# A decoder layer on one Trainium2 core: seven- and eight-product units of gate and up alternate, and a group's sums and transpositions move

## The chip, the cores and the metric

One core of one Trainium2 chip runs the whole kernel. The metric is the device time of one execution in microseconds. Three timed executions of the kernel before took 1185.75, 1186.57 and 1187.09 us; the median is 1186.57.

## The reference

One layer of a hybrid decoder on 256 tokens of width 2048, all in float32. What the change touches is the SwiGLU part, whose hidden width is 5632:

```python
def swiglu(h, w_gate, w_up, w_down):
    g = jnp.einsum('bsd,df->bsf', h, w_gate)
    u = jnp.einsum('bsd,df->bsf', h, w_up)
    return jnp.einsum('bsf,fd->bsd', jax.nn.silu(g) * u, w_down)

h = layer_norm(ALPHA * h + m, ln1_g, ln1_b)     # m: RG-LRU heads and differential attention
h = layer_norm(ALPHA * h + swiglu(h, ...), ln2_g, ln2_b)
h = layer_norm(ALPHA * h + sigmoid(h @ w_ple_gate + b) * (p @ w_ple_proj), ln3_g, ln3_b)
```

## The kernel before

**Precision.** Every float32 operand is split into two parts, hi (rounded to fp32r) and lo (what is left). A product of two matrices is three matmuls: hi by hi, hi by lo, lo by hi (`product`, L851 to L856). For the weights ScalarE casts the hi half `wh` (L159) and VectorE subtracts to get the lo half `wl` (L150). For some halves, listed in `by_dma`, VectorE is spared: ScalarE writes `wl = -wh` (L161), and a DMA issued by GpSimd adds `w` to it in place (L162).

**Stream.** All weights pass through one object, `Stream`, in units of 1 MB (128 x 2048 values). `load` (L98) issues a unit's load on SyncE's queue into one of 3 buffers `w`. A load waits until everything that read the buffer's last unit is done, and these are the casts, the subtractions and, for a `by_dma` half, GpSimd's accumulating DMA. A unit has two halves of 1024 columns, each with its `wh` and `wl` in one of 6 buffers. The program calls `tick` after each stretch of matmuls; a tick lets each running job (a generator) emit its next step and then prepares at most one lo and one hi of the stream, as long as the hi is no more than 6 halves past what the matmuls had freed a tick earlier (`room`, L166). Engines take their instructions in the order in which they were emitted.

**Gate and up.** The hidden width is cut into 11 groups of 512 columns, in three parts of 4, 4 and 3 groups (`FPARTS`), each part followed by its share of the down projection. A group has 8 units (`PAIRS`), one for each 256 rows of the contraction, with gate and up together. Five are normal units ("N" below): 8 products, 24 matmuls, a tick after each quarter (6 matmuls). Three (`SEVEN`, "S" below) are done with 7 products in place of 8, in the manner of Strassen: 21 matmuls and four ticks. They need four weight operands: the unit's first half, a block of 512 columns, and two halves of sums that VectorE makes from the loaded unit (`add_up`, L128). The order in a group is N N N N N S S S; the second halves of units 2, 3 and 4 are `by_dma`. Four PSUM banks `q[h][g]` hold plain results (token half h; g is gate or up); p1, p6, p5 and p7 hold products that enter more than one result.

**Finish.** At the first tick of the last S unit, `finish` (L912) starts: it copies the banks out, adds the products, applies SiLU, multiplies, and 3 ticks later transposes the two token halves on TensorE (L950). ScalarE and VectorE then write the transposed hi and lo into `hT`, the input of the down projection. Its steps run beside the first N units of the next group.

Of the kernel before, what the change touches and what calls it, by code (L numbers as in the profile page):

```python
# [12 lines left out]
F32R = mybir.dt.float32r  # L13
BF16 = mybir.dt.bfloat16
AF = mybir.ActivationFunctionType
ALU = mybir.AluOpType
# [4 lines left out]
P = 128  # L21
D = 2048
S = 256
KT = D // P
# [24 lines left out]
NSM = 32 + 8 * 4 + 1 + 64  # L49
PAIRS = KT // 2  # L50
SEVEN = 3


class Stream:
# [152 lines left out]
def tile_hybrid_layer(ctx: ExitStack, tc: tile.TileContext, t: dict):  # L207
    nc = tc.nc
# [3 lines left out]
    act = ctx.enter_context(tc.tile_pool(name="act", bufs=1))  # L212
# [5 lines left out]
    srcs = [t["w_a"][b] for b in range(NB)]  # L218
# [6 lines left out]
    sevens, by_dma = set(), set()  # L225
    for f0, nf in FPARTS:
        for f in range(f0, f0 + nf, 4):
            sevens.update(range(len(srcs) + PAIRS - SEVEN, len(srcs) + PAIRS))
            by_dma.update((len(srcs) + m, 1) for m in range(PAIRS - SEVEN - 3, PAIRS - SEVEN))
            srcs += [tuple(t[w][f:f + 4, :, 2 * P * j:2 * P * (j + 1)].rearrange("f p c -> p f c")  # L230
                           for w in ("w_gate", "w_up")) for j in range(PAIRS)]
        srcs += [t["w_down"][f0 // 4 + kq, blk] for kq in range(nf // 4) for blk in range(2)]
        srcs += [t["w_down"][f0 // 4 + kq, blk] for blk in range(2, 4) for kq in range(nf // 4)]
    srcs += [t["w_pg"][blk, kq] for blk in range(4) for kq in range(4)]
    after_load = {}
    st = Stream(nc, wp, srcs, after_load, sevens, by_dma)

    def bank(name):
        return pm.tile([P, 512], F32, tag="mm", name=name)

    def aux(name):
        return pa.tile([P, 512], F32, tag="aux", name=name, bufs=2)
# [81 lines left out]
    ident = const.tile([P, P], F32, name="ident")  # L324
# [28 lines left out]
    for (k0, n), x in zip(XCHUNKS, x8):  # L353
        c = slice(k0 * P, (k0 + n) * P)
# [3 lines left out]
    first = [bank("xr") for _ in range(FIRST)]  # L358
    n0 = st.take(FIRST)
    for (k0, n), x in zip(XCHUNKS, x8):  # L360
        ks = slice(k0, k0 + n)
        st.split(xhl[:, ks, :S], xhl[:, ks, S:], x)
        for u in range(FIRST):
            c = slice(k0 * P, (k0 + n) * P)
# [293 lines left out]
    for i in range(4):  # L658
        c = slice(i * 512, (i + 1) * 512)
# [8 lines left out]
    def tmp(name):  # L668
        return late.tile([P, 512], F32, tag="tmp", name=name, bufs=7)
# [142 lines left out]
    x1 = act.tile([P, KT, 2 * S], F32R, tag="B", name="x1")  # L812
    xsum = []

    def sums_of_x1():

        xsum.append(late.tile([P, SEVEN, 4, 2, P], F32R, tag="gb", name="xsum"))
        work = act.tile([P, 2 * SEVEN * 512], F32, tag="A", name="work")  # L820
        x, sums = work[:, :SEVEN * 512], work[:, SEVEN * 512:]
        ks = slice(KT - 2 * SEVEN, KT)
        nc.vector.tensor_tensor(x.rearrange("p (k s) -> p k s", s=S), x1[:, ks, :S].bitcast(F32),
# [27 lines left out]
    def product(ps, a, w, first, last):  # L851

        out = ps.rearrange("p (f c) -> p f c", c=P)
        nc.tensor.matmul(out, a[0], w[0], start=first, stop=False)  # L854
        nc.tensor.matmul(out, a[0], w[1], start=False, stop=False)  # L855
        nc.tensor.matmul(out, a[1], w[0], start=False, stop=last)  # L856

    def operand(n, j, i):

        parts = st.half(n, j)  # L860
        if n in st.sevens and j:
            return [w[:, i * 512:(i + 1) * 512].rearrange("p (f c) -> p f c", c=P) for w in parts]
        return [w.rearrange("p (f k c) -> p f k c", f=4, k=2)[:, :, i, :] for w in parts]

    def gate_up(hT, i0):

        n0 = st.take(PAIRS)  # L870
        q = [[bank("gu") for _ in range(2)] for _ in range(2)]
        for m in range(PAIRS - SEVEN):
            for g in range(2):
                for h in range(2):
                    for i in range(2):
                        k = 2 * m + i
                        a = [x1[:, k, o + h * P:o + (h + 1) * P] for o in (0, S)]
                        product(q[h][g], a, operand(n0 + m, g, i), m + i == 0,
                                g * h * i == 1 and m == PAIRS - SEVEN - 1)
                    st.free(h)  # L880
                    st.tick()
        pp = [aux("p1"), aux("p6")]
        both = pa.tile([P, 2, 512], F32, tag="sc", name="p57")
        p1, p6, p5, p7 = pp[0], pp[1], both[:, 0, :], both[:, 1, :]
        for m in range(PAIRS - SEVEN, PAIRS):
            n, first, last = n0 + m, m == PAIRS - SEVEN, m == PAIRS - 1
            def x(h, i):
                return [x1[:, 2 * m + i, o + h * P:o + (h + 1) * P] for o in (0, S)]
            def sx(i):
                return [xsum[0][:, m - PAIRS + SEVEN, i, a, :] for a in range(2)]  # L890
            product(q[0][0], x(0, 1), operand(n, 0, 1), False, last)
            product(p1, x(0, 0), operand(n, 0, 0), first, last)
            if last:
                if hT is None:
                    hT = act.tile([P, KT, 2 * S], F32R, tag="A", name="hT")
                st.start(finish(hT, i0, q, p1, p6, p5, p7))
            st.free()
            st.tick()
            product(q[0][1], sx(3), operand(n, 1, 0), False, last)
            st.free()  # L900
            product(p5, sx(0), operand(n, 2, 0), first, last)
            st.tick()
            product(p7, sx(1), operand(n, 2, 1), first, last)
            st.free()
            product(q[1][0], x(1, 1), operand(n, 3, 1), False, last)
            st.tick()
            product(p6, sx(2), operand(n, 3, 0), first, last)
            st.free()
            st.tick()
        return hT  # L910

    def finish(hT, i0, q, p1, p6, p5, p7):  # L912


        add = lambda out, a, b, op=ALU.add: nc.vector.tensor_tensor(out, a, b, op)
        yield
        g0 = tmp("g0")
        nc.scalar.copy(g0, q[0][0])
        yield
        u0, u1 = tmp("u0"), tmp("u1")  # L920
        nc.scalar.copy(u0, q[0][1])
        add(g0, p1, g0)
        nc.scalar.copy(u1, q[1][1])
        yield
        g1, u2, u3 = tmp("g1"), tmp("u2"), tmp("u3")
        nc.scalar.copy(g1, q[1][0])
        nc.scalar.copy(u2, p6)
        yield
        add(u2, p1, u2)
        nc.scalar.activation(g0, g0, AF.Silu)  # L930
        yield
        add(u3, p7, u2)
        yield
        add(u2, p5, u2)
        add(g1, g1, u3)
        yield
        add(u3, p5, u3)
        nc.scalar.activation(g1, g1, AF.Silu)
        yield
        add(u0, u0, u2, ALU.subtract)  # L940
        yield
        add(u1, u1, u3, ALU.subtract)
        add(g0, g0, u0, ALU.mult)
        yield
        add(g1, g1, u1, ALU.mult)
        yield 3
        for h, g in enumerate((g0, g1)):
            tp = aux("tp")
            for i in range(4):
                nc.tensor.transpose(tp[:, i * P:(i + 1) * P], g[:, i * P:(i + 1) * P], ident)  # L950
            yield
            tp = tp.rearrange("p (a b) -> p a b", b=P)
            hi, lo = (hT[:, i0:i0 + 4, o + h * P:o + (h + 1) * P] for o in (0, S))
            nc.scalar.copy(hi, tp)
            yield
            nc.vector.tensor_tensor(lo, tp, hi.bitcast(F32), ALU.subtract)

    for part, (f0, nf) in enumerate(FPARTS):
        hT = None
        for i0 in range(0, nf, 4):  # L960
            hT = gate_up(hT, i0)
        nq = nf // 4
        end = part == len(FPARTS) - 1
        if end:
            gb = load_gb(2)
        two = [[bank("dps") for _ in range(2)] for _ in range(2)]
        for kq in range(nq):
            for blk in range(2):
                token_major(two[blk], hT, kq, kq == 0, kq == nq - 1)
        for blk in range(4):  # L970
            if blk < 2:
                st.start(residuals(blk, two[blk], part == 0, stats if end else None), 1 + 2 * blk)
                continue
            ps = [bank("dps") for _ in range(2)]
            if end and blk == 3:
                x2 = act.tile([P, KT, 2 * S], F32R, tag="B", name="x2")
                token_major(ps, hT, 0, True, False)
                token_halves(ps, hT, (1, 2), False, True, norm_to(NORM2, x2, ps, False, stats, gb, ln_cols[2]))
                continue
            for kq in range(nq):  # L980
                token_major(ps, hT, kq, kq == 0, kq == nq - 1)
            st.start(residuals(blk, ps, part == 0, stats if end else None))
# [46 lines left out]
    n = st.take(4)  # L1029
# [126 lines left out]
```

## Time and profile before

| what | value |
|---|---|
| median of three timed executions | 1186.57 us |
| profiled execution | 1187.35 us |
| its span (first to last instruction) | 1185.6 us |
| TensorE matmul busy | 1161.7 us, 98% |
| VectorE busy | 877.7 us, 74% |
| ScalarE busy | 681.2 us, 57% |
| granted TensorE clock, mean | 0.995 |
| accumulating DMAs wl<-w | 33 of 512 KB |

The profile lists busy time by engine and by line, the chain that ended last, and waits with what released them. Matmuls overlap: each is recorded with some 0.39 us while the next starts 0.23 us after it, so a matmul's cost is the distance between two starts. A stall shorter than the overlap doesn't appear as idle time; it is seen in the starts.

### The profile page before, as it was taken

The numbers are of one execution on the slowest core, as the hardware profiler recorded it, in microseconds if no ns is written. First come the engines' busy times: TensorE is split into PE (matmuls) and PEld (weight loads), VectorE is DVE, ScalarE is ACT, GpSimd is POOL, SyncE is SP. The second block draws the span as 40 slices with busy tenths as digits, with TensorE's granted clock in tenths as the row PEclk, the third lists the DMA queues.
The fourth block names the chain that finished last, engine by engine and source line by source line (L and its number), as shares of the span: only waits on it lengthen the run. The fifth ranks groups of instructions, "written<-read, shape, count | busy, mean of one in ns | idle before, by whom it ended". The sixth has DMA issues, their size and how long they took to land.

```text
span 1185.6 us, 14774 instructions
## 1 busy us (share of the span) xinstructions
PE 1161.7 (98%) x5495; PEld 963.7 (81%) x5495; DVE 877.7 (74%) x1160; ACT 681.2 (57%) x968; POOL 65.0 (5%) x97
## 2 busy tenths in 40 slices
PE   9999999999999999999999999999999999999995
PEld 7888888888887777877888888888888888877885
DVE  6975987885667967968544887787545797866877
ACT  6767666664456747746334756764345775635540
POOL 0000000001011000000000000000000000002001
PEclk9999999999999999999999999999999999999998
DMA  9756454447738788776557779766558877846741
GB/s 327 257 223 214 146 181 172 176 144 267 274 117 259 250 225 221 242 213 249 180 207 212 199 232 266 216 219 244 191 180 228 228 232 218 315 179 220 303 150 72
DMA packets 124456, 256.29 MB, mean 216 GB/s; under 512 B 6433, under 2 KB 100553, under 8 KB 108385
## 3 DMA queue, kind: packets, MB, share of 16 engines
q1 hardware_dynamic: 116208, 221.52, 54.0%
q0 software_dynamic: 8176, 33.84, 11.8%
q8 instruction: 43, 0.70, 0.2%
q14 instruction: 29, 0.23, 0.1%
HBM read 233.82 MB, written 5.78 MB: 202 GB/s over the span
## 4 chain that ended last, share of the span: by engine, by line
PE 77%; DVE 10%; DMA 7%; issue 3%; ACT 1%; POOL 1%; SPq 0%; DVEq 0%; POOLq 0%; ACTq 0%
PE gu L856 7%; PE gu L854 7%; PE gu L855 7%; PE dps L277 6%; PE dps L279 6%; PE dps L278 6%; DMA w<-in_w_up 4%; DVE wl L150 4%; PE ops L278 2%; PE xr L251 2%; PE ops L279 2%; PE ops L277 2%; PE k L251 2%; PE yg L251 2%; DVE sums L130 2%
## 5 line engine op out<-in xcount | busy, mean ns | idle before, releaser
L159 ACT CAST wh<-w 128x1024 fp32r<-128x1024 f32 (+1 forms) x404 | 407.7, 1017 | 276.2 <-PE dps L279 117.7
L150 DVE TENSOR_TENSOR wl<-w,wh 128x1024 fp32r<-128x1024 f32 (+1 forms) x371 | 432.0, 1173 | 154.0 <-ACT wh L159 153.7
L855 PE MATMUL gu<-wl,x 128*128 128x512 f32 x506 | 197.8, 391 | 2.5 <-DVE wl L150 1.4
L854 PE MATMUL gu<-wh,x 128*128 128x512 f32 x506 | 198.9, 393 | 0.0
L856 PE MATMUL gu<-wh,x 128*128 128x512 f32 x506 | 197.3, 390 | 0.0
L277 PE MATMUL dps<-wh,hT 128*128 128x512 f32 x352 | 138.2, 393 | 1.4 <-DVE z L699 1.0
L279 PE MATMUL dps<-wh,hT 128*128 128x512 f32 x352 | 137.2, 390 | 0.0
L278 PE MATMUL dps<-wl,hT 128*128 128x512 f32 x352 | 137.2, 390 | 0.0
L855 PEld LDWEIGHTS gu<-wl,x 128*128 128x128 f32 x506 | 95.1, 188 | 23.7 <-DVE wl L150 3.1
L159 ACT CAST wh<-sums 128x1024 fp32r<-128x1024 f32 x66 | 68.9, 1052 | 76.6 <-DVE sums L130 51.5
L856 PEld LDWEIGHTS gu<-wh,x 128*128 128x128 f32 x506 | 95.1, 188 | 19.9
L854 PEld LDWEIGHTS gu<-wh,x 128*128 128x128 f32 x506 | 95.1, 188 | 19.3
L130 DVE TENSOR_TENSOR sums<-w 128x1024 f32<-128x1024 f32 x33 | 40.3, 1221 | 79.1 <-DMA w<-in_w_up 79.1
L150 DVE TENSOR_TENSOR wl<-sums,wh 128x1024 fp32r<-128x1024 f32 x66 | 77.9, 1220 | 9.8 <-ACT wh L159 9.7
L277 PEld LDWEIGHTS dps<-wh,hT 128*128 128x128 f32 x352 | 66.1, 188 | 16.6 <-issue 2.3
L279 PEld LDWEIGHTS dps<-wh,hT 128*128 128x128 f32 x352 | 66.1, 188 | 13.9
L278 PEld LDWEIGHTS dps<-wl,hT 128*128 128x128 f32 x352 | 66.2, 188 | 13.3
L162 POOL DMA_DIRECT2D wl<-w x33 | 28.5, 863 | 605.3 <-ACT wl L161 385.6
L277 PE MATMUL ops<-wh,mhl 128*128 128x512 f32 x128 | 50.4, 394 | 0.0
L278 PE MATMUL ops<-wl,mhl 128*128 128x512 f32 x128 | 49.9, 390 | 0.0
L279 PE MATMUL ops<-wh,mhl 128*128 128x512 f32 x128 | 49.9, 390 | 0.0
L251 PE MATMUL xr<-xhl,wh 128*128 128x512 f32 x128 | 47.3, 411 | 1.7 <-ACT wh L78 1.7
(257 smaller groups left out, 2008.6 us busy)
## 6 DMA issues: line engine op xcount, KB each, us to landing
w<-in_w_gate SPq DMA_DIRECT2D x88, 512.0 KB, 3.7
w<-in_w_up SPq DMA_DIRECT2D x88, 512.0 KB, 5.3
w<-in_w_down SPq DMA_DIRECT2D x44, 1024.0 KB, 4.8
w<-in_w_a SPq DMA_DIRECT2D x28, 1024.0 KB, 4.9
wl<-w POOLq DMA_DIRECT2D x33, 512.0 KB, 5.9
w<-in_w_out SPq DMA_DIRECT2D x16, 1024.0 KB, 4.8
w<-in_w_pg SPq DMA_DIRECT2D x16, 1024.0 KB, 4.9
w<-in_w_v SPq DMA_DIRECT2D x8, 1024.0 KB, 4.9
```

Of the source, the lines that this page charges most:

```text
L130: add = lambda out, a, b: self.nc.vector.tensor_tensor(out, a, b, ALU.add)
L150: self.nc.vector.tensor_tensor(wl, src, wh.bitcast(F32), ALU.subtract)
L159: self.nc.scalar.copy(self.shaped(wh, src, cols), src)
L162: self.nc.gpsimd.dma_start(wl, src, accum_op=ALU.add)
L251: nc.tensor.matmul(ps, wh[:, c], xhl[:, k, :], start=(k == 0), stop=False)
L277: nc.tensor.matmul(ps, ah, wh[:, c], start=first, stop=False)
L278: nc.tensor.matmul(ps, ah, wl[:, c], start=False, stop=False)
L279: nc.tensor.matmul(ps, al, wh[:, c], start=False, stop=last)
L854: nc.tensor.matmul(out, a[0], w[0], start=first, stop=False)
L855: nc.tensor.matmul(out, a[0], w[1], start=False, stop=False)
L856: nc.tensor.matmul(out, a[1], w[0], start=False, stop=last)
```

## The change

The units of a group come in another order. A group is now S N S N S N N N (`ORDER`); only the very first group is N N N N S N S N (`ORDER0`). In every group but the first, both halves of the N units at positions 1 and 3 are `by_dma`, and no others. The three shared products are complete after the last S unit, so `add_products` starts there: one copy and four adds. Two ticks after its adds it runs the transpositions of the group before, which were separate steps at the end of `finish`. `combine` takes the four banks out beside the last N unit, starting with its first quarter. After a part's last group the transpositions start with the sixth tick of the down projection. `hT` is taken at the second group of a part.

```diff
+ORDER = (("S", 5), ("N", 0), ("S", 6), ("N", 1), ("S", 7), ("N", 2), ("N", 3), ("N", 4))
+ORDER0 = (("N", 0), ("N", 1), ("N", 2), ("N", 3), ("S", 5), ("N", 4), ("S", 6), ("N", 7))
...
-            sevens.update(range(len(srcs) + PAIRS - SEVEN, len(srcs) + PAIRS))
-            by_dma.update((len(srcs) + m, 1) for m in range(PAIRS - SEVEN - 3, PAIRS - SEVEN))
...
+            for i, (kind, j) in enumerate(ORDER if f else ORDER0):
+                if kind == "S":
+                    sevens.add(len(srcs))
+                elif f and i in (1, 3):
+                    by_dma.update(((len(srcs), 0), (len(srcs), 1)))
...
+        for pos, (kind, m) in enumerate(order):
+            n, first, last = n0 + pos, pos == first_s, pos == last_s
+            if kind == "N":
+                for g in range(2):
+                    for h in range(2):
...
+                        if pos == PAIRS - 1 and g + h == 0:
+                            st.start(combine(q, sums))
+                        st.free(h)
+                        st.tick()
+                continue
...
             product(p6, sx(2), operand(n, 3, 0), first, last)
+            if last:
+                st.start(add_products(sums, p1, p6, p5, p7, before))
...
+    def add_products(sums, p1, p6, p5, p7, before):
+        c1, u2, u3, u4 = (sums.setdefault(i, tmp(i)) for i in ("c1", "u2", "u3", "u4"))
+        nc.scalar.copy(c1, p1)
+        yield
+        add(u2, p6, c1)
+        yield
+        add(u3, p7, u2)
+        yield
+        add(u2, p5, u2)
+        yield
+        add(u4, p5, u3)
+        if before is not None:
+            yield 2
+            yield from before
+
+    def combine(q, sums):
+        g0, g1, u0 = (sums.setdefault(i, tmp(i)) for i in ("g0", "g1", "u0"))
+        u1 = sums["u4"]
         nc.scalar.copy(g0, q[0][0])
         yield
+        nc.scalar.copy(g1, q[1][0])
+        add(g0, g0, sums["c1"])
+        yield
         nc.scalar.copy(u0, q[0][1])
+        add(g1, g1, sums["u3"])
+        yield
+        add(u1, q[1][1], u1, ALU.subtract)
         nc.scalar.activation(g0, g0, AF.Silu)
         yield
+        add(u0, u0, sums["u2"], ALU.subtract)
         nc.scalar.activation(g1, g1, AF.Silu)
         yield
         add(g0, g0, u0, ALU.mult)
         yield
         add(g1, g1, u1, ALU.mult)
...
         for i0 in range(0, nf, 4):
+            if i0 == 4:
+                hT = act.tile([P, KT, 2 * S], F32R, tag="A", name="hT")
+            before = gate_up(i0, ORDER if f0 + i0 else ORDER0, before and before(hT))
+        st.start(before(hT), 6)
```

## Rows read from the trace of the kernel before

**Rows 1.** The page: busy time by engine, and the granted clock in 40 slices.

```profile
PE 1161.7 (98%) x5495; PEld 963.7 (81%) x5495; DVE 877.7 (74%) x1160; ACT 681.2 (57%) x968; POOL 65.0 (5%) x97
PEclk9999999999999999999999999999999999999998
```

**Rows 2.** Timeline of TensorE, an N unit: start us, duration us, line, out<-in.

```profile
680.35 0.39 PE L856 MATMUL gu<-wh,x 128*128 128x512 f32 x1
680.58 0.39 PE L854 MATMUL gu<-wh,x 128*128 128x512 f32 x1
```

**Rows 3.** Chain, TensorE's transpositions (first of each pair), by start: start us, us.

```profile
682.11 0.44 PE tp L950 x4
...
724.57 0.44 PE tp L950 x4
...
809.90 0.44 PE tp L950 x4
```

**Rows 4.** Timeline of TensorE, the same transpositions for groups 0 to 3.

```profile
418.55 0.49 PE L950 MATMUL tp<-ident,g 128*128 128x128 f32 x3
...
464.36 0.49 PE L950 MATMUL tp<-ident,g 128*128 128x128 f32 x3
...
506.83 0.38 PE L950 MATMUL tp<-ident,g 128*128 128x128 f32 x2
...
551.81 0.38 PE L950 MATMUL tp<-ident,g 128*128 128x128 f32 x2
```

**Rows 5.** Timeline of TensorE, two stalls; in brackets idle time and its releaser.

```profile
446.99 0.50 PE L855 MATMUL gu<-wl,xsum 128*128 128x512 f32 x1 [0.28 <-DVE wl L150]
...
379.33 0.39 PE L854 MATMUL gu<-wh,x 128*128 128x512 f32 x1
380.74 0.50 PE L855 MATMUL gu<-wl,x 128*128 128x512 f32 x1 [1.02 <-DMA wl<-w]
```

**Rows 6.** Lines of VectorE in group 5 (668.0 to 710.5): count, busy us, mean ns.

```profile
L150 DVE TENSOR_TENSOR wl<-sums,wh 128x1024 fp32r<-128x1024 f32 x6 | 7.1, 1219 | 0.1
L130 DVE TENSOR_TENSOR sums<-sums,w 128x512 f32<-128x512 f32 x6 | 4.1, 688 | 0.1
L130 DVE TENSOR_TENSOR sums<-w 128x1024 f32<-128x1024 f32 x3 | 3.7, 1221 | 7.4 <-DMA w<-in_w_up 7.4
```

**Rows 7.** Timeline of ScalarE from the boundary of groups 4 and 5.

```profile
670.90 0.66 ACT L930 ACTIVATE g<-g 128x512 f32<-128x512 f32 x1
671.43 1.07 ACT L159 CAST wh<-w 128x1024 fp32r<-128x1024 f32 x1
672.53 1.06 ACT L161 ACTIVATE wl<-wh 128x1024 fp32r<-128x1024 f32 x1
673.50 1.04 ACT L159 CAST wh<-w 128x1024 fp32r<-128x1024 f32 x1
```

**Rows 8.** Timeline of GpSimd, the same group: the three accumulating DMAs.

```profile
673.88 0.86 POOL L162 DMA_DIRECT2D wl<-w  x1 [32.66 <-PE gu L855]
677.39 0.86 POOL L162 DMA_DIRECT2D wl<-w  x1 [2.64 <-ACT wl L161]
681.86 0.86 POOL L162 DMA_DIRECT2D wl<-w  x1 [3.61 <-ACT wl L161]
```

**Rows 9.** Timeline of SyncE's queue, the same stretch: the loads.

```profile
678.95 0.37 SPq L105 DMA_DIRECT2D w<-in_w_gate  x1
...
683.45 0.37 SPq L105 DMA_DIRECT2D w<-in_w_gate  x1
...
689.92 0.37 SPq L105 DMA_DIRECT2D w<-in_w_gate  x1
```

**Rows 10.** Waits of SyncE's queue: us in total, times, longest us.

```profile
SPq L105 <- DMA wl<-w: 162.9, 33, 9.1
```

**Rows 11.** Tile wl on GpSimd: issue to landing of all 33.

```profile
DMA to landing us min/median/max: 4.5/5.9/10.8
```

**Rows 12.** Chain before the stalls of group 3: start us, us, what.

```profile
505.14 10.67 DMA w<-in_w_up
```

More of the change, by code (lines that the diff above doesn't have):

```diff
@@ L227, in tile_hybrid_layer @@
         for f in range(f0, f0 + nf, 4):
-            sevens.update(range(len(srcs) + PAIRS - SEVEN, len(srcs) + PAIRS))
-            by_dma.update((len(srcs) + m, 1) for m in range(PAIRS - SEVEN - 3, PAIRS - SEVEN))
-            srcs += [tuple(t[w][f:f + 4, :, 2 * P * j:2 * P * (j + 1)].rearrange("f p c -> p f c")
-                           for w in ("w_gate", "w_up")) for j in range(PAIRS)]
+            for i, (kind, j) in enumerate(ORDER if f else ORDER0):
[3 more added lines that the diff above has]
+                    by_dma.update(((len(srcs), 0), (len(srcs), 1)))
+                srcs.append(tuple(t[w][f:f + 4, :, 2 * P * j:2 * P * (j + 1)].rearrange("f p c -> p f c")
+                                  for w in ("w_gate", "w_up")))
         srcs += [t["w_down"][f0 // 4 + kq, blk] for kq in range(nf // 4) for blk in range(2)]
@@ L863, in operand, with gate_up @@
         return [w.rearrange("p (f k c) -> p f k c", f=4, k=2)[:, :, i, :] for w in parts]
-    def gate_up(hT, i0):
+    def gate_up(i0, order, before):
         n0 = st.take(PAIRS)
         q = [[bank("gu") for _ in range(2)] for _ in range(2)]
[L872 to L881, printed above, removed]
         pp = [aux("p1"), aux("p6")]
@@ L884, in gate_up @@
         p1, p6, p5, p7 = pp[0], pp[1], both[:, 0, :], both[:, 1, :]
-        for m in range(PAIRS - SEVEN, PAIRS):
-            n, first, last = n0 + m, m == PAIRS - SEVEN, m == PAIRS - 1
+        kinds = [kind for kind, _ in order]
+        first_s, last_s = kinds.index("S"), PAIRS - 1 - kinds[::-1].index("S")
+        sums = {}
+        for pos, (kind, m) in enumerate(order):
[3 more added lines that the diff above has]
+                    for h in range(2):
+                        for i in range(2):
+                            a = [x1[:, 2 * m + i, o + h * P:o + (h + 1) * P] for o in (0, S)]
+                            product(q[h][g], a, operand(n, g, i), pos + i == 0 or (pos == 1 and first_s == 0 and
+                                    (h, g) == (1, 1) and i == 0), pos == PAIRS - 1 and i == 1)
+                        if pos == PAIRS - 1 and g + h == 0:
[3 more added lines that the diff above has]
+                continue
             def x(h, i):
@@ L890, in sx @@
                 return [xsum[0][:, m - PAIRS + SEVEN, i, a, :] for a in range(2)]
-            product(q[0][0], x(0, 1), operand(n, 0, 1), False, last)
+            product(q[0][0], x(0, 1), operand(n, 0, 1), pos == 0, False)
             product(p1, x(0, 0), operand(n, 0, 0), first, last)
[L893 to L896, printed above, removed]
             st.free()
             st.tick()
-            product(q[0][1], sx(3), operand(n, 1, 0), False, last)
+            product(q[0][1], sx(3), operand(n, 1, 0), pos == 0, False)
             st.free()
@@ L904, in gate_up, with add @@
             st.free()
-            product(q[1][0], x(1, 1), operand(n, 3, 1), False, last)
+            product(q[1][0], x(1, 1), operand(n, 3, 1), pos == 0, False)
             st.tick()
             product(p6, sx(2), operand(n, 3, 0), first, last)
+            if last:
+                st.start(add_products(sums, p1, p6, p5, p7, before))
             st.free()
             st.tick()
-        return hT
-    def finish(hT, i0, q, p1, p6, p5, p7):
-        add = lambda out, a, b, op=ALU.add: nc.vector.tensor_tensor(out, a, b, op)
-        yield
[L917 to L930, printed above, removed]
+        return lambda hT: transposed(hT, i0, sums)
+    def add(out, a, b, op=ALU.add):
+        nc.vector.tensor_tensor(out, a, b, op)
+    def add_products(sums, p1, p6, p5, p7, before):
+        c1, u2, u3, u4 = (sums.setdefault(i, tmp(i)) for i in ("c1", "u2", "u3", "u4"))
+        nc.scalar.copy(c1, p1)
+        yield
+        add(u2, p6, c1)
         yield
@@ L934, in finish @@
         add(u2, p5, u2)
-        add(g1, g1, u3)
         yield
-        add(u3, p5, u3)
+        add(u4, p5, u3)
[5 more added lines that the diff above has]
+        u1 = sums["u4"]
+        nc.scalar.copy(g0, q[0][0])
+        yield
+        nc.scalar.copy(g1, q[1][0])
+        add(g0, g0, sums["c1"])
+        yield
+        nc.scalar.copy(u0, q[0][1])
+        add(g1, g1, sums["u3"])
+        yield
+        add(u1, q[1][1], u1, ALU.subtract)
+        nc.scalar.activation(g0, g0, AF.Silu)
+        yield
+        add(u0, u0, sums["u2"], ALU.subtract)
         nc.scalar.activation(g1, g1, AF.Silu)
         yield
-        add(u0, u0, u2, ALU.subtract)
-        yield
-        add(u1, u1, u3, ALU.subtract)
         add(g0, g0, u0, ALU.mult)
@@ L945, in finish, with transposed @@
         add(g1, g1, u1, ALU.mult)
-        yield 3
-        for h, g in enumerate((g0, g1)):
+    def transposed(hT, i0, sums):
+        for h, g in enumerate(("g0", "g1")):
             tp = aux("tp")
             for i in range(4):
-                nc.tensor.transpose(tp[:, i * P:(i + 1) * P], g[:, i * P:(i + 1) * P], ident)
+                nc.tensor.transpose(tp[:, i * P:(i + 1) * P], sums[g][:, i * P:(i + 1) * P], ident)
             yield
@@ L958, in tile_hybrid_layer @@
     for part, (f0, nf) in enumerate(FPARTS):
-        hT = None
+        before = None
         for i0 in range(0, nf, 4):
-            hT = gate_up(hT, i0)
+            if i0 == 4:
+                hT = act.tile([P, KT, 2 * S], F32R, tag="A", name="hT")
+            before = gate_up(i0, ORDER if f0 + i0 else ORDER0, before and before(hT))
+        st.start(before(hT), 6)
         nq = nf // 4
```

## The prediction

> **What bounds the kernel now.** I read the page first: TensorE is busy for 98% of the span and the granted clock is at its full level, 2.4 GHz, in all slices but the last, which reads 8 tenths [rows 1]. So a change that leaves the matmuls as they are can win only stalls between them. Next I read TensorE's timeline in an undisturbed unit, for the price of a matmul: the starts lie 0.225 to 0.23 us apart [rows 2]; I use 0.227. An N unit is then 24 x 0.227 = 5.44 us (a quarter 1.36), an S unit 21 x 0.227 = 4.76, and a group 5 x 5.44 + 3 x 4.76 = 41.5 plus two sets of transpositions of 0.44. The third view is the transpositions, which stand at the same place of every group and so measure its length. In the second part one group lasts 42.46 us and three together 127.79 [rows 3], 0.4 more than three times that: hardly a stall is left there. In the first part the lengths are 45.81, 42.47 and 44.98 [rows 4], so groups 1 and 3 lose 3.35 and 2.5. Last, the stalls themselves [rows 5]: in S units a matmul with `wl` waits for VectorE, and a matmul behind a wait is recorded with 0.50 us in place of 0.39, a restart of 0.11. In group 0 one wait for an accumulating DMA costs 380.74 - 379.33 - 0.227 = 1.18, with its restart 1.3; for its S units I estimate a half of what group 1 loses, 1.6. Together 2.9. Sum of what could be won: 2.9 + 3.35 + 2.5 = 8.8 us, less than 1%.
>
> **The change part by part.**
>
> Matmuls and transpositions: a group keeps 3 S and 5 N units, 183 matmuls and 8 transpositions. Nothing.
>
> The alternation. VectorE's sums and their `wl` are 7.1 + 4.1 + 3.7 = 14.9 us for three S units [rows 6], 5.0 for one, and the `wl` of its own two blocks (1024 and 512 columns, like 1.22 and 0.69 there) makes 6.9. Three in a row are 20.7 us against 14.3 of TensorE, which is how a late load turns into stalls. Alternating with an N unit whose halves go by DMA, it is 6.9 against 10.2. These stalls go. In group 0 VectorE makes two more `wl` than before (no `by_dma` there: five N units without DMA, but one fewer half before the first S), right behind the norm, so I count half of its 2.9: gain 1.5 + 3.35 + 2.5 = 7.4 (between 5 and 8.8).
>
> Finish: VectorE keeps 10 adds and products; ScalarE has one copy fewer and one more L161 (1.06 [rows 7]) for each group, 4 `by_dma` halves instead of 3. VectorE saves one `wl` (1.22). Neither engine is full; nothing by itself. The banks: the next group's first S unit rewrites q00 at once, q01 after 6 matmuls (1.36 us). The copy of q01 is done at -0.7 (below), so this is covered by 2 us; without that cover it would cost up to a copy, which I take as long as a SiLU, 0.53 between two starts [rows 7].
>
> The lead of the accumulating DMAs. This is what is late next. Before, the halves concerned are the second ones of N units and come behind other N halves: the cast is emitted some 12 us ahead of its use (first quarter of unit 0 to third quarter of unit 2). Now, by the limit of 6 halves, the cast of position 1's first half is emitted behind the third quarter of the last N unit, one quarter and one S unit before its use: 1.36 + 4.76 = 6.1 us. The other three halves have the same 6.1. The chain that must fit, from rows: start of the cast to start of L161 1.10, L161 1.06, its end to the issue 0.29 [rows 7, 8], issue to landing at least 4.5 [rows 11]: 6.95. It doesn't fit. Step by step, with t = 0 the start of a group's first S unit:
>
> - *Position 1, first half.* q01 ends at -1.36, and its copy stands ahead of the cast in ScalarE's queue: start -1.2 (a matmul ends 0.16 after the next start), step 0.53, cast at -0.67, L161 from 0.43 to 1.49, issue 1.78. Nothing else is moving then (the next load waits for this unit's DMA, below), so the landing is as for a group's first DMA, which let a load go 678.95 - 673.88 = 5.07 after its issue [rows 8, 9], some 0.1 behind the landing; between this and the shortest, 4.5, I take 4.8: 6.58. The second matmul needs it at 4.76 + 0.23 = 4.99: **1.6 late**.
> - *Second half.* Behind L161 (step 0.97 [rows 7]) stand two SiLUs of 0.53: cast at 2.46, L161 ends 4.62, issue 4.91, landing 9.71. Need 4.99 + 2.72 = 7.71: **2.0 late** in all, with two restarts of 0.11: 2.2 us a group. By the shortest landing it is 1.7 without restarts, by the median of 5.9 3.1.
> - *Position 3.* Its buffer comes free when position 1's first half is used up: 4.76 + 2.72 + 1.6 + 0.16 = 9.24; ScalarE comes to it at about 9.0 (from 4.6 on three casts of about 0.95, the last behind VectorE's second sums, which I put at 8). Cast 9.24, L161 ends 11.4, issue 11.7. By now loads move: SyncE's queue waits for the accumulating DMA of the unit whose buffer it refills (33 waits, 162.9 us before [rows 10]; in [rows 9] each of the three loads is one that waited so), so position 4's unit is issued at 9.8 and the next about 1 us later. An accumulating DMA beside such loads took 689.92 - 681.86 - 0.1 = 8.0 [rows 8, 9]; I take 7.7, between it and the median, by the nearer row: landing 19.4. Need: 4.76 + 5.44 + 4.76 + 0.23 = 15.19, and 2.2 of position 1: 17.4. **2.0 late**, with the restart 2.1. If the loads don't disturb it (4.8) it is in time: 0. If it takes 9, 3.4. Its second half lands about 22 against 22.2: nothing.
>
> The copy and the SiLUs stand ahead only where a group follows a group: 8 of 10. Where one follows the down projection (groups 4 and 8), the cast is at -2.6 and the landing at 4.7, in time; position 3 stays late by as much. Sum: 8 x 2.2 + 10 x 2.1 - 7.4 = **+31.2 us**. The profiled execution had 1187.35 (1185.6 of span and 1.75 around it), so 1218.6 on its scale; the median lies 0.8 lower: 1217.8, **1218**.
>
> A rule that bears on the landing, apart from the sum: in the Trainium skill, "DMA: Bandwidth & Descriptors", section on the anatomy of one DMA on the GpSimd path, a DMA takes about 2.0 us plus its bytes at 436 GB/s, which for 512 KB is an estimate of 3.2 us. By that, the sum would be that of the rival A below. The trace disagrees for this form: none of 33 landed under 4.5 [rows 11]. The same page (section "SWDGE vs HWDGE vs iDMA") says that each DMA engine takes turns between the queues fed by GpSimd and by the hardware generators; the 8.0 us beside loads agrees.
>
> **The rivals.**
>
> A. *The DMAs are in time, and only the stalls of S units go.* Place: position 1 and 3 of ten groups; deciding point: a loss under 7.4 / 10 = 0.74 us a group. If a landing took 3.2, position 1 would be 0.1 late in its first half and 0.4 in its second, with restarts 0.6, position 3 in time: 8 x 0.6 - 7.4 = -2.6, time 1184; with no wait at all 1179. For it: DMAs are quiet while these run. Against: the shortest landing in the trace is 4.5, and with it position 1 is still 1.7 late.
>
> B. *Position 3 isn't late.* The loads of 9.8 and 10.8 don't slow its DMA. 8 x 2.2 - 7.4 = +10: 1197. For it: second DMAs of a group, issued shortly before a load, took 683.45 - 677.39 - 0.1 = 6.0 [rows 8, 9]. Against: here two loads are issued ahead of the DMA, not behind.
>
> C. *The loads come late too.* Position 4's unit is loaded only after position 1's DMA. Beside accumulating DMAs such a load took 10.67 us, and the group that it fed is one of the stalled ones [rows 12, 4]. From 9.8 it lands at 20.5; VectorE's work up to the `wl` of the first sums is 1.22 + 1.22 + 1.38 + 0.69 + 1.22 = 5.7 [rows 6], so 26.2 against a need at 26.7 (15.19 + 4.1 of waits and restarts so far + 5.44, and 2.04 into the S unit). A spare of 0.5 us: if it goes, each group loses another 3, as groups 1 and 3 did. +31 + 30: about 1248.
>
> **How the numbers follow.** My forecast 0.58, B 0.21, C 0.13, A 0.08. The forecast's own range is 1205 to 1232 (position 1 at 1.7 to 3.3, position 3 at 1 to 3). With B below and part of C above, the range is 1194 to 1238. About 0.2% (2.4 us) is what a measurement of this kernel can tell from no change. Faster comes only from A with short landings: 0.07; same, its border, 0.02; slower 0.91: even the shortest landings with position 3 in time give 8 x 1.9 - 8.8 = +6.
>
> **What would show it.** In the profile after: waits of gu L855 for DMA wl<-w, 18 to 30 of them, 20 to 40 us together; groups that last 45 to 48 us, but 42.5 to 44 for group 0; hardly a wait of L855 for VectorE's `wl`; landings of 4.5 to 5 and of 7 to 8 us. Wrong if groups 5 to 7 last 42.5, or if L855 waits for VectorE instead. A granted clock below full speed after the waits would be a cost that I have not counted: before, 1.02 us of idle left it at its full level.

## The result, and the profile after

The changed kernel takes 1261.13 us (median; 1260.82 to 1261.74) against 1186.16 of the kernel before in the same runs: a ratio of 1.0638, with a 95% interval of 1.0616 to 1.066. It is slower by 75 us. The forecast was 1218, with a range up to 1238: the direction and the place were right, the size was not, and the range missed.

The page after, busy time by engine and the 40 slices of TensorE, its clock and GpSimd:

```profile
PE 1187.8 (94%) x5498; PEld 978.8 (78%) x5498; DVE 874.2 (69%) x1148; ACT 684.2 (54%) x962; POOL 70.6 (6%) x104
...
PE   9999999999999898899998898899998898999996
...
PEclk9999999999999898899999898999999998999998
```

Against [rows 1], TensorE has gone from 98% to 94%, and its clock is no longer full in six slices of the gate and up stage, in or next to which TensorE is less busy too. The waits of TensorE (us in total, times, longest) name one cause:

```profile
PE gu L860 <- DMA wl<-w: 51.7, 18, 4.8
PE p L859 <- DVE u L924: 0.9, 1, 0.9
```

Eighteen waits are 8 + 10, the count that was forecast: 8 at position 1, 10 at position 3. Before there was one, of 1.0 us [rows 5]. No wait of L860 for VectorE's `wl` is left. The transpositions, which measure a group, in the second part (start us, duration):

```profile
735.08 0.49 PE L970 MATMUL tp<-ident,g 128*128 128x128 f32 x3
...
786.47 0.38 PE L970 MATMUL tp<-ident,g 128*128 128x128 f32 x2
...
838.06 0.38 PE L970 MATMUL tp<-ident,g 128*128 128x128 f32 x2
```

A group takes 51.4 to 51.6 us, where it took 42.46 [rows 3]. TensorE's timeline in group 5 shows the two waits and what follows the second:

```profile
697.61 0.39 PE L859 MATMUL gu<-wh,x 128*128 128x512 f32 x1
699.19 0.50 PE L860 MATMUL gu<-wl,x 128*128 128x512 f32 x1 [1.20 <-DMA wl<-w]
...
709.64 0.39 PE L859 MATMUL gu<-wh,x 128*128 128x512 f32 x1
714.03 0.80 PE L860 MATMUL gu<-wl,x 128*128 128x512 f32 x1 [4.00 <-DMA wl<-w]
714.62 0.63 PE L861 MATMUL gu<-wh,x 128*128 128x512 f32 x1
715.05 0.63 PE L859 MATMUL gu<-wh,x 128*128 128x512 f32 x1
```

By starts, less one step of 0.227, position 1 waits 1.35 us and position 3 4.16. Behind the second wait the starts lie 0.43 apart, not 0.227. Two stretches of the same group by windows (busy time of each engine, then granted clock) show why:

```profile
713.30:720.00 6.70, 5.97 (x14) 4.76 (x15) 1.44 (x2) 0.87 (x1) 0.00 (x0) 0.50 0.69 176
720.10:748.90 28.80, 28.80 (x132) 23.82 (x131) 22.56 (x26) 17.14 (x23) 0.84 (x1) 1.00 0.67 207
```

For some 6 us of work the granted clock is 0.50, which is 1.2 GHz, and 14 matmuls ran where 26 would have: 2.8 us lost. In this group it fell while TensorE waited, and rose again while it worked. Then why the DMA of position 3 is late: GpSimd's and SyncE's queues in this group.

```profile
694.61 0.84 POOL L164 DMA_DIRECT2D wl<-w  x1 [35.05 <-PE p L861]
697.70 0.85 POOL L164 DMA_DIRECT2D wl<-w  x1 [2.24 <-ACT wl L163]
704.46 0.84 POOL L164 DMA_DIRECT2D wl<-w  x1 [5.91 <-ACT wl L163]
```

```profile
702.34 0.37 SPq L107 DMA_DIRECT2D w<-in_w_gate  x1
...
703.36 0.44 SPq L107 DMA_DIRECT2D w<-in_w_gate  x1
...
716.79 0.37 SPq L107 DMA_DIRECT2D w<-in_w_gate  x1
...
717.82 0.44 SPq L107 DMA_DIRECT2D w<-in_w_gate  x1
```

As forecast, a load waits for the accumulating DMA of the unit in its buffer; the next load in the queue is ready by then, and the two go out 1 us apart. Position 3's DMA, issued 1.1 us behind the second load at 704.46, is used at 714.03: 9.5 us. The landings of all 40 fall into two groups, 4.5 to 5.1 us for the 20 of position 1 and 8.5 to 10.4 for the 20 of position 3; before, the median was 5.9 [rows 11]:

```profile
DMA to landing us min/median/max: 4.5/6.8/10.4
```

Summing the start distances over one step of 0.227 through the gate and up stage of both profiled executions: the 8 waits at position 1 are 11.6 us, the 10 at position 3 are 43.0, and the matmuls at half clock lost 23.4. A new wait between groups 0 and 1 (p for u, in the waits above) is 1.0. In group 0, which has two S and six N units now, three matmuls were added (5498 against 5495 on the pages): 0.7. Less the 8.8 us of stalls that are gone this is 71; the rest of the 74.4 us by which the profiled executions differ (1261.74 and 1187.35) is restarts and small steps.

### The profile page after: what moved, and what is told of

It reads as the page before. It is cut to its first block, busy times and chain, and to the rows that moved or that the text cites. A ratio compares the mean times of both kernels' runs of the same rounds, so it can differ in the third digit from the quotient of the medians.

```text
span 1259.8 us, 14752 instructions
## 1 busy us (share of the span) xinstructions
PE 1187.8 (94%) x5498; PEld 978.8 (78%) x5498; DVE 874.2 (69%) x1148; ACT 684.2 (54%) x962; POOL 70.6 (6%) x104
## 4 chain that ended last, share of the span: by engine, by line
PE 73%; DMA 12%; DVE 7%; issue 5%; ACT 1%; POOL 1%; SPq 0%; POOLq 0%; DVEq 0%; ACTq 0%
DMA wl<-w 10%; PE gu L860 8%; PE gu L861 7%; PE gu L859 7%; PE dps L282 6%; PE dps L284 6%; PE dps L283 6%; PE ops L282 2%; PE ops L284 2%; PE ops L283 2%; DVE wl L152 2%; PE xr L256 2%; PE k L256 2%; PE yg L256 2%; PE q L256 2%
## 5 line engine op out<-in xcount | busy, mean ns | idle before, releaser
L152 DVE TENSOR_TENSOR wl<-w,wh 128x1024 fp32r<-128x1024 f32 x364 | 425.5, 1174 | 224.6 <-ACT wh L161 222.8
L860 PE MATMUL gu<-wl,x 128*128 128x512 f32 x512 | 212.8, 416 | 52.0 <-DMA wl<-w 51.7
L859 PE MATMUL gu<-wh,x 128*128 128x512 f32 x512 | 209.4, 409 | 0.0
L861 PE MATMUL gu<-wh,x 128*128 128x512 f32 x512 | 208.3, 407 | 0.0
L860 PEld LDWEIGHTS gu<-wl,x 128*128 128x128 f32 x512 | 101.8, 199 | 83.2 <-DMA wl<-w 62.6
L861 PEld LDWEIGHTS gu<-wh,x 128*128 128x128 f32 x512 | 102.2, 200 | 21.6
L859 PEld LDWEIGHTS gu<-wh,x 128*128 128x128 f32 x512 | 101.5, 198 | 22.2
L164 POOL DMA_DIRECT2D wl<-w x40 | 34.0, 849 | 651.3 <-PE p L861 297.2
```

The source lines that it names most:

```text
L152: self.nc.vector.tensor_tensor(wl, src, wh.bitcast(F32), ALU.subtract)
L164: self.nc.gpsimd.dma_start(wl, src, accum_op=ALU.add)
```

## The experiments

The theory: accumulating DMAs that are started too close to their use make TensorE wait, two loads let go together make position 3 the worse of the two, and the long waits halve the clock.

### No accumulating DMA

```diff
-                elif f and i in (1, 3):
-                    by_dma.update(((len(srcs), 0), (len(srcs), 1)))
```

> No half goes by an accumulating DMA; VectorE makes every wl; order of units and the new finish as in the changed kernel. Theory (the halves at positions 1 and 3 are started too late, and the long waits at position 3 halve the clock): the 18 waits for DMA wl<-w and all 0.5-clock stretches of the gate and up parts go, groups last 42.5 to 43, total 1179 to 1187. Rival (the alternating order itself loads VectorE or the load queue too much): waits of L860 for VectorE's wl take their place, over 1 us a group, total above 1195.

Measured: 1178.73 us, 0.9934 (0.9918 to 0.995) of the kernel before, so 0.7% under the kernel before and 82 us under the changed one. The clock is full up to the last slices, and no wait for a `wl` is left in gate and up, only the one between groups 0 and 1. Two transpositions in the second part:

```profile
693.84 0.38 PE L968 MATMUL tp<-ident,g 128*128 128x128 f32 x2
...
736.31 0.38 PE L968 MATMUL tp<-ident,g 128*128 128x128 f32 x2
```

A group takes 42.47 us, as in the best ones before. So the whole loss hangs on the four halves by DMA, and the order and the new finish cost next to nothing by themselves.

### The DMAs at positions 6 and 7

```diff
-                elif f and i in (1, 3):
+                elif f and i in (6, 7):
```

> The same four halves of a group go by DMA, but at positions 6 and 7 (N units behind N units) in place of 1 and 3. Walking the order of the stream through, their casts come 9.5 to 13.6 us ahead of use instead of 7.5. Theory (lead, not number): no wait for DMA wl<-w over 0.5 us, no 0.5-clock stretch, total 1177 to 1184. Rival (four accumulating DMAs a group are too many wherever they stand, since each holds the load queue): the loads of the next group's first units come late, waits of L859 or L860 for casts or wl behind loads, total above 1195.

Measured: 1198.73 us, 1.0103 (1.0086 to 1.012). A miss: better than positions 1 and 3 by 62 us, but the rival's bound of 1195 is passed too. TensorE's waits:

```profile
PE gu L860 <- DMA wl<-w: 8.0, 7, 2.1
PE dps L282 <- ACT g L947: 4.0, 2, 3.3
```

Seven waits for DMAs are left, and a new one: where a part ends, ScalarE stands at a cast whose load was held by these DMAs, and behind it are the copies that free the banks for the down projection. The longest of these, 3.5 us by starts at the end of the third part, was followed by a stretch at 0.50, which the theory had excluded too. The four DMAs go out 2 to 2.5 us apart and in group 1 took 8.4 to 9.8 us each. The landings were no shorter than in the changed kernel (5.9 to 10.0 us, median 7.7 against 6.8), so it is lead that took most of the waits away; but four DMAs in a row aren't hidden there either.

### Position 1 only

```diff
-                elif f and i in (1, 3):
+                elif f and i in (1,):
```

> Only position 1 goes by DMA, position 3 by VectorE. Theory: 8 waits of 1.2 us idle (1.36 to 1.9 by starts) at position 1 stay, those of position 3 go, and with them the clock stretches: 1186 + 8 x 1.5 - 7 = about 1191 (1187 to 1196), no 0.5-clock stretch between 300 and 1100 us. Rival (the clock falls by any wait, also 1.4 us): stretches of 0.5 stay, total above 1205.

Measured: 1194.06 us, 1.0063 (1.0045 to 1.008). The eight waits are there (10.3 us idle, the longest 1.6), those of position 3 are gone, and the clock stays full. As the theory had it: waits of up to 1.6 us didn't lower the clock in this run.

### Work in place of waiting

```diff
             if kind == "N":
+                if pos == 3 and first_s == 0:
+                    for _ in range(18):
+                        nc.tensor.matmul(q[0][0], zero[:, :P], zero, start=False, stop=False)
```

> The changed kernel with 18 more matmuls (128x128 by 512, bf16 zeros added to q00) ahead of the first product of position 3 in ten groups: 4.1 us of TensorE work in place of the 3.7 to 4.9 us of waiting; the output is the same. Theory (the clock halves because TensorE waits for over 4 us): the clock stays at 1.0 and the 23 us that matmuls lost at half clock come back: 1261 - 23 + up to 8 = 1236 to 1248, although 180 matmuls are added. Rival (the half clock has another cause, a limit on the work of the stage or the alternation of units): the stretches stay and the total is 1261 or more, up to 1261 + 41 if the fill isn't hidden.

Measured: 1240.7 us, 1.0457 (1.0437 to 1.0476): 180 matmuls more than the changed kernel, and 20 us less. The granted clock of the stage, here and then in the changed kernel (the column behind POOL):

```profile
360.00:1100.00 740.00, 721.87 (x3194) 571.98 (x3192) 495.10 (x538) 404.74 (x452) 36.20 (x44) 1.00 0.71 216
```

```profile
360.00:1150.00 790.00, 735.70 (x3146) 596.87 (x3145) 515.38 (x561) 412.34 (x463) 36.44 (x45) 0.96 0.69 209
```

So it is the waiting that lowers the clock, not the order or the load of the stage. The sum agrees with the 23 us that the starts gave: the fill took 39.0 us (180 starts 0.2165 apart) and left 8.2 us of the 43.0 of waiting, which alone would make 1265; the time is 25 us less.

### Position 3 only

```diff
-                elif f and i in (1, 3):
+                elif f and i in (3,):
```

> Only position 3 goes by DMA, position 1 by VectorE. Theory (the DMA of position 3 is slow because two loads, let go together by position 1's DMA, are ahead of it): nothing holds those loads now, they go earlier and one at a time; issue to landing 4.5 to 7 us, wait 0 to 1.9 us, no 0.5-clock stretch before 1100 us, total 1179 to 1196. Rival (the DMA at position 3 is late and slow in its own right): landing over 9 us, waits over 4, half clock, total above 1215.

Measured: 1205.5 us, 1.0162 (1.014 to 1.0184), between the two. The landings are as the theory had them, 4.5 to 6.0 us. But the waits were eight of 1.6 to 4.2 us by starts, and behind three of them (4.15, 2.34 and 2.55 us) the clock fell to 0.50, where the theory had none. In group 7 ScalarE and TensorE show why position 3 is late:

```profile
771.02 1.05 ACT L161 CAST wh<-sums 128x1024 fp32r<-128x1024 f32 x1 [2.01 <-DVE sums L132]
771.98 1.04 ACT L161 CAST wh<-w 128x1024 fp32r<-128x1024 f32 x1
773.05 1.06 ACT L163 ACTIVATE wl<-wh 128x1024 fp32r<-128x1024 f32 x1
```

```profile
777.10 0.39 PE L859 MATMUL gu<-wh,x 128*128 128x512 f32 x1
779.93 0.50 PE L860 MATMUL gu<-wl,x 128*128 128x512 f32 x1 [2.44 <-DMA wl<-w]
```

The cast of position 3 starts only 5.1 us ahead of the unit's first matmul at 777.10: it stands behind a cast that waits for VectorE's sums (VectorE has position 1's `wl` to make as well, which I take for the reason). So position 3 needs no slow DMA to be late; ScalarE's queue can do it. My expectation had only the buffer in mind.

### One load in place of two

```diff
-            if isinstance(self.srcs[n], tuple):
+            if n in self.skipped:
+                self.nc.gpsimd.memset(w, 0.0)
+            elif isinstance(self.srcs[n], tuple):
...
+                if f and i == 5:
+                    skipped.add(len(srcs))
```

> The changed kernel, but the load of the unit at position 5 (1 MB, ten groups) is left out and its buffer set to zero by GpSimd, so that part of the product is missing; all else is the same. Only one load then runs beside position 3's DMA, as beside a third DMA of a group in the kernel before. Theory (the second load makes the difference between 7.7 us and 9.5): landing 7 to 8 us, wait at position 3 1.5 to 2.8 us, no half clock, total 1208 to 1228, about the forecast of 1218. Rival (not the load): landing 9 us or more, half clock stays, total above 1245.

Measured: 1200.39 us, 1.0123 (1.0101 to 1.0144). All landings, and position 3 of group 5:

```profile
DMA to landing us min/median/max: 4.5/4.7/6.9
```

```profile
685.01 0.39 PE L864 MATMUL gu<-wh,x 128*128 128x512 f32 x1
686.33 0.50 PE L865 MATMUL gu<-wl,x 128*128 128x512 f32 x1 [0.93 <-DMA wl<-w]
```

Without the second load no DMA takes over 6.9 us (10.4 in the changed kernel), the wait at position 3 falls from 4.16 to 1.09 us, and the clock stays full. In the ten groups, position 3 has six waits of 0.8 to 1.4 us and four times none. The total is below what I expected: beside this one load, issued 1.9 to 2.7 us ahead of it, position 3's DMA took 4.7 to 6.9 us, not 7 to 8. That isn't a price for every single load: in the kernel before, the DMA issued at 634.93, with one load issued 0.8 us ahead of it and no other load until it landed, took

```profile
DMA to landing us min/median/max: 7.6/7.6/7.6
```

What the distance between load and DMA does was not tested by itself.

### The old order without DMAs

```diff
-            by_dma.update((len(srcs) + m, 1) for m in range(PAIRS - SEVEN - 3, PAIRS - SEVEN))
```

> The kernel before (N N N N N S S S, old finish) with no half by accumulating DMA. Theory (alternating spares VectorE, so without DMAs the old order falls behind in three S units in a row): waits of L855 for VectorE's wl of 0.5 to 3 us in most groups, groups over 43, total 1183 to 1200. Rival (the DMAs, which hold the loads, were the only cause of the stalls before, and the order plays no part): all groups at 42.5 and a total of 1177 to 1180, like the run without DMAs in the new order.

Measured: 1177.02 us, 0.992 (0.9902 to 0.9939): the rival's number. Transpositions of groups 0 to 3, to set beside [rows 4], then VectorE's two largest lines over one group's length, 672.0 to 714.5 (busy us, mean ns, idle before and its releaser):

```profile
414.94 0.38 PE L949 MATMUL tp<-ident,g 128*128 128x128 f32 x2
...
457.41 0.27 PE L949 MATMUL tp<-ident,g 128*128 128x128 f32 x1
...
499.87 0.38 PE L949 MATMUL tp<-ident,g 128*128 128x128 f32 x2
...
542.35 0.38 PE L949 MATMUL tp<-ident,g 128*128 128x128 f32 x2
```

```profile
L150 DVE TENSOR_TENSOR wl<-w,wh 128x1024 fp32r<-128x1024 f32 (+1 forms) x17 | 18.9, 1126 | 0.4 <-ACT wh L159 0.4
L150 DVE TENSOR_TENSOR wl<-sums,wh 128x1024 fp32r<-128x1024 f32 x6 | 7.2, 1222 | 3.7 <-ACT wh L159 3.7
```

Groups 1 to 3, which lost 3.35, 0 and 2.5 us [rows 4], now take 42.46 to 42.48 like all others, with three S units in a row and VectorE making every `wl`. So the stalls before came with the DMAs, and S units in a row alone don't make them. That the DMAs did it by holding and slowing the loads is read from [rows 10, 12]; no run separates the two. The run without DMAs in the new order is 1.7 us longer, as much as its three more matmuls in group 0 and its wait between groups 0 and 1 add up to.

### The casts ahead of the copy and the SiLUs

```diff
     def tick(self, prepare=True):
+        if self.ahead:
+            self.prepare()
+            prepare = False
         for job in list(self.jobs):
...
+            st.ahead = pos in (0, PAIRS - 1)
```

> The changed kernel, but in the ticks of a group's first and last unit the stream prepares ahead of the jobs, so the casts of position 1 stand before the copy of q01 and the SiLUs in ScalarE's queue. Theory (those three instructions are what makes position 1 late): the 8 waits of 1.4 us at position 1 go or fall under 0.3, position 3 stays, total 1245 to 1254. Rival (the 6 halves of lead are too short in any order): waits over 1 us stay at position 1, total 1257 to 1264.

Measured: 1251.51 us, 1.0544 (1.0516 to 1.0572). TensorE at position 1 of group 5, and the wait at position 3 behind it:

```profile
696.33 0.39 PE L862 MATMUL gu<-wh,x 128*128 128x512 f32 x1
696.56 0.50 PE L863 MATMUL gu<-wl,x 128*128 128x512 f32 x1
...
706.96 0.39 PE L862 MATMUL gu<-wh,x 128*128 128x512 f32 x1
712.58 0.80 PE L863 MATMUL gu<-wl,x 128*128 128x512 f32 x1 [5.23 <-DMA wl<-w]
```

Here the second matmul follows the first after 0.23 us. Of the eight waits at position 1 two are left, of 1.2 and 0.4 us. So what stood ahead in ScalarE's queue made that wait, not the 6 halves alone. Position 3 gave a part back (46.0 us in ten waits, where it was 43.0): its DMA met the same two loads, and its use now came sooner.

## Why the prediction was wrong

**The mechanism and the count** were right: 18 waits of the second matmul for DMA wl<-w, at the two places named, 8 and 10. Without the DMAs they are all gone.

**Position 1**: forecast 1.6 late in the first half and 2.0 in all, 2.2 with restarts; measured 1.35 in group 5, and 1.46 with the restart (1.44 on the mean of eight, without); the second half cost nothing. Landings were 4.54 and 4.52 us in group 5, where I had taken 4.8. The run with the casts ahead shows that the chain through ScalarE's queue was read rightly. The term was 17.6 us for eight groups and measured 11.6 and restarts.

**Position 3, the step that failed first**: "An accumulating DMA beside such loads took 8.0; I take 7.7". The row was one of a DMA beside one load, with the next issued behind it. Here two loads were ahead, as the prediction itself had written ("position 4's unit is issued at 9.8 and the next about 1 us later"), and I priced them like one. The rest of the chain held: in group 5 the DMA was issued 11.6 us after the group's start, where 11.7 was forecast. But it took 9.5, so the wait was 4.3 on the mean of ten and not 2.0: 43.0 us, where the term was 21. With one of the loads left out it is at most 1.4.

**The clock, the second failure**: a term of 0 that measured 23.4. "A granted clock below full speed after the waits would be a cost that I have not counted" named it, but the row behind it showed only 1.02 us of idle, a quarter of what came. A better row was in the same trace, and [rows 1] was misread: a 9 there stands for nine tenths or more, not for the full clock. In the kernel before, TensorE waited 1.74 us in the first stage, and the window behind it (busy times by engine, then the clock) has 0.50:

```profile
9.56 0.68 PE L251 MATMUL xr<-xhl,wh 128*128 128x512 f32 x1 [1.74 <-ACT wh L78]
```

```profile
9.70:13.10 3.40, 3.40 (x11) 2.74 (x12) 2.71 (x7) 2.56 (x7) 0.00 (x0) 0.50 1.06 369
```

I should have carried the clock as a rival with a price (half the matmuls of the stretch behind each wait); then the range would have reached further up. The Trainium skill has the rule on the page "TensorE: Matmul & The Clock Gate", section on HAM oscillation, that a matmul kernel which waits for a slice of data in each pass can start every pass at the lower clock. The trace agrees: ten groups, ten stretches at 0.50, each begun within the long wait or within 1 us of its end, and none when matmuls filled it. I didn't weigh it, since the waits that I forecast were half as long.

**The gain of 7.4** was right in size, by luck: its reason isn't borne out. The run without DMAs is 7.5 us under the kernel before (1186.21 in the same runs), but so is, by 8.8 (against 1185.83), the old order without them. What the kernel before paid for went with the DMAs alone, without alternating; whether alternating would have saved it with the old DMAs kept was not run. My "three in a row are 20.7 us against 14.3" left out that the stream may be prepared up to 6 halves ahead. **"A group keeps 3 S and 5 N units"** overlooked group 0, which cost the 0.7 us of three more matmuls.

**Rivals.** A fell: no landing under 4.5. B fell: position 3 was late in all ten groups. C fell: loads did come behind accumulating DMAs, yet no S unit waited for `wl` from VectorE. **Not foreseen**: the wait of 1.0 us at the end of group 0, where the next group's first S unit rewrites a bank that `add_products` is still reading.

## What to carry to other kernels

Before giving work to a DMA, add up its whole chain (what stands ahead in each engine's queue, the issue, the landing beside the loads that will then be moving) against the lead that the buffers allow; and see what the DMA holds up by reading a buffer that a load is waiting for. A wait that may last several microseconds on the busiest engine is priced twice, once for itself and once for the clock behind it. And when a kernel is to be relieved by an offload, run it once without the offload: here both orders were faster with none.

## What the hardware showed that I had not expected

An accumulating DMA of 512 KB landed in 4.5 to 5.1 us with hardly anything else moving (position 1 of the changed kernel), in 4.7 to 6.9 behind one load of 1 MB issued about 2 us ahead (one load in place of two), in 7.6 and 7.7 behind one issued 0.8 us ahead (twice in the kernel before), and in 8.5 to 10.4 behind two issued 1 us apart (position 3 of the changed kernel). In these runs the granted clock was 0.50 behind every wait of TensorE of 3.5 us or more by starts, for a stretch that cost up to 2.8 us. For shorter waits there is no one bound: the 1.74 us of idle in the kernel before were followed by 0.50, 1.7 us of idle before 461.79 in the changed kernel by 1.00; and in the run with position 3 alone, two waits of much the same length, at 686 and at 777 us, were followed by 0.50 and by 1.00:

```profile
686.20:689.00 2.80, 0.62 (x3) 0.20 (x3) 2.70 (x4) 1.59 (x4) 0.24 (x1) 1.00 1.01 192
689.60:692.90 3.30, 3.30 (x9) 2.56 (x8) 2.09 (x2) 0.36 (x1) 0.00 (x0) 0.50 0.33 70
777.00:780.00 3.00, 0.56 (x4) 0.14 (x2) 2.85 (x4) 1.79 (x4) 0.29 (x1) 1.00 1.04 197
780.00:784.00 4.00, 4.00 (x18) 3.31 (x19) 2.69 (x4) 1.86 (x2) 0.00 (x0) 1.00 0.37 71
```

What tells the two apart stays open.
